# Raw weight blocks in the cached pages' buffers, and 30 turns of the identity, at the start of a hybrid decoder step

## The chip, the core and the metric

The kernel runs on one core of a Trainium2 chip. The core has five engines that run at the same time and wait for one another through semaphores: TensorE (PE in the profile, with its weight loads as PEld), VectorE (DVE), ScalarE (ACT), GpSimd (POOL), and SyncE (SP), which issues most of the transfers between the chip's memory and the core's own buffers. The metric is the device time of one execution in microseconds, lower is better.

## The reference, cut to what matters

One decoder layer is computed for a prompt of 1024 tokens and for 64 sample tokens (8 sequences of 8) that attend to 8192 cached positions each. Its beginning is a norm, one combined projection whose columns are split, and the low-rank latents:

```
n = rmsnorm(h, lw['g_mix'])
u = n @ lw['w_in']
gq, gk, gv, gg, ga, mq, mkv, mkr = jnp.split(u, split_points, axis=-1)
...
cq = rmsnorm(mq, lw['mla_g_qa'])
qf = (cq @ lw['mla_w_qup']).reshape(B, T, MLA_HEADS, MLA_NOPE + MLA_ROPE)
...
ckv = rmsnorm(mkv, lw['mla_g_kva'])
krope = rope(rmsnorm(mkr, lw['mla_g_kr']), pos)
```

The columns `ga, mq, mkv, mkr` are the last 432 of `w_in` (16 + 256 + 128 + 32); the program calls them the latents. After this come gated linear attention and latent attention, whose sample part runs over the paged cache, then an output projection, a gated MLP with a causal convolution, and a gated per-layer embedding.

## The kernel before

Every product is computed in float32 accuracy out of two halves: a value is cast to a rounded high half (`act.copy`) and the remainder is the low half (a subtraction on DVE or POOL); three matmuls (high by high, high by low, low by high) make one product. A weight therefore comes in four steps: a transfer into a raw buffer, a cast on ACT, a subtraction on DVE or POOL, and only then the matmuls.

The program is written as generators that are advanced in turns: the dense work of the prompt in two halves of 512 tokens (`prompt_half`), and the sample sequences' attention over the cached pages. A scheduler then fixes the order of instructions on each engine at build time, by program order, by priority (`tc.high_priority` raises the sample's q chain) and by when buffers come free. Each engine runs its list strictly in that order, so an instruction that waits holds all behind it on its engine. SP can hold eight transfers under way; a ninth waits for the first to land.

The beginning of the first half does this. `sample_x` (L335) loads the 64 sample rows (tile `xin_s`) and the gains `gmix`, normalises the rows and turns them on TensorE (`pt`, L132) into `xTs`. `load_x` (L751) loads the prompt's rows in tiles of 128, the first two into `lat`, the next two into `xin`; each is squared and summed on ACT (L122), scaled by POOL (L108, L111) and DVE (L125), turned on TensorE (L132) and split into `xTh` and `xTl` (L115, L116). `load_lat` (L259) brings the latents' weights in eight blocks of 128 by 432: a raw tile (`stage`, three buffers), a cast to `w` on ACT (L267), a subtraction (L271) on POOL for odd blocks and on DVE for even ones, into `chl` or `w`. `sample_u` (L343) multiplies the sample rows by them: 16 matmuls into `ps_sm`. `proj_lat` multiplies each of four prompt tiles by them: 24 matmuls into `ps_lt` for each (both at L278).

Then comes the sample's q chain: the latents' norm, `ps_qs` (L390), sums and norms on ACT and DVE (L163 to L331), the turns `pt_q` (L416), `ps_qp` (L420), `pt_qr` (L426), and on POOL the operands of the paged attention (L484 to L491). Beside it runs `mix`: chunks of 128 columns of `w_in` (`ps_pj`, L139 to L141), whose raw halves go through the same three `stage` buffers. The paged attention turns pages (`craw`, three buffers of 128 by 1024) into `ctp` and `ks`; `csq` (two buffers of 128 by 1024) holds its squares.

Of the kernel before, what the change touches and what calls it, by code (L numbers as in the profile page):

```python
# [8 lines left out]
F32 = mybir.dt.float32  # L9
# [9 lines left out]
P = 128  # L19
# [20 lines left out]
NL = 432  # L40
# [4 lines left out]
def step_kernel(ctx: ExitStack, tc: tile.TileContext, A):  # L45
    nc = tc.nc
    pe, act, dve, pool, sp = nc.tensor, nc.scalar, nc.vector, nc.gpsimd, nc.sync
# [4 lines left out]
    def ctile(shape, dt, name):  # L52
        return const.tile(shape, dt, name=name, tag=name)
# [3 lines left out]
    ident = ctile([P, P], F32, "ident")  # L57
# [18 lines left out]
    def load_constants():  # L76
        for nm in gains:
            sp.dma_start(gains[nm], A[nm][0].partition_broadcast(P))
        dve.scalar_tensor_tensor(gqk, gains["mla_g_qn"], SCALE, gains["mla_g_kn"], ALU.mult, ALU.mult)
        dve.tensor_scalar(gains["mla_g_qr"], gains["mla_g_qr"], SCALE, None, ALU.mult)  # L80
        sp.dma_start(ropes, A["rope_s"])
# [37 lines left out]
    def norm_rows(wk, x, rows, gb, out=None):  # L119
        junk = wk.tile([P, D], BF16, tag="sqd", name="junk", bufs=1)  # L120
        ss = wk.tile([P, 1], F32, tag="ss", name="ss")
        act.activation(junk[:rows], x, AF.Square, scale=1.0 / 32.0, accum_out=ss[:rows])  # L122
        r = rstd(wk, ss[:rows], rows, 1)
        out = x if out is None else out
        dve.scalar_tensor_tensor(out, x, r[:rows, 0:1], gb[:rows], ALU.mult, ALU.mult)  # L125
        return out

    def transpose_split(ps, xs, rows, put, here=False):
        for c0 in (0, 4):
            pt = ps([P, 4, P], "pt")  # L130
            for c in range(4):
                m = pe.transpose(pt[:, c, :rows], xs[:rows, (c0 + c) * P:(c0 + c + 1) * P], ident[:rows, :rows])  # L132
                if here and c0 == c == 0:
                    tc.keep_in_program_order(m)
            hi, lo = put(c0)
            split(hi, lo, pt[:, :, :rows])
# [47 lines left out]
    cp = ph1.enter_context(tc.tile_pool(name="cp", bufs=1, side="right"))  # L184
# [7 lines left out]
    def pm(shape, name):  # L192
        return psM.tile(shape, F32, tag="m", name=name)

    def cst(shape, dt, name):
        return cp.tile(shape, dt, name=name, tag=name)
# [6 lines left out]
    chl = [cst([P, 9, 258], F32R, "chl")]  # L203
# [28 lines left out]
    wp = den.enter_context(tc.tile_pool(name="wp", bufs=3))  # L232
# [4 lines left out]
    def wtile():  # L237
        return wp.tile([P, 2 * D], F32R, tag="w", name="w")
# [17 lines left out]
        hl = wload(wp, w_in[:, c0:c0 + P], 8, P, "w", sbufs=3, lo_eng=lo_eng, out=(w[:, :, 0], w[:, :, 1]))  # L256
        return hl + (w,)

    def load_lat(first, lo_eng=pool):  # L259

        w = [wtile()[:, 0:4 * NL].rearrange("p (k c) -> p k c", c=NL) for _ in range(3)]
        hi = [w[k // 4][:, k % 4] for k in range(8)]
        lo = first + [w[2][:, k] for k in range(4)]
        for k in range(8):
            raw = wp.tile([P, NL], F32, tag="stage", name="stage", bufs=3)
            sp.dma_start(raw, w_in[k * P:(k + 1) * P, O_GA:O_GA + NL])
            act.copy(hi[k], raw)  # L267
            r, h_ = raw, hi[k].bitcast(F32)
            if len(lo[k].shape) == 3:
                r, h_ = (x.rearrange("p (a c) -> p a c", a=2) for x in (r, h_))  # L270
            (lo_eng if k % 2 else dve).tensor_tensor(lo[k], r, h_, ALU.subtract)  # L271
        return hi, lo
# [63 lines left out]
    def sample_x():  # L336
        x = wk.tile([P, D], F32, tag="xin", name="xin_s")
        sp.dma_start(x[:R], A["x_sample"].rearrange("b t d -> (b t) d"))
        sp.dma_start(gmix, A["g_mix"][0].partition_broadcast(P))
        norm_rows(wk, x[:R], R, gmix)  # L340
        transpose_split(pm, x, R, lambda c0: (xTs[:, c0:c0 + 4, 0:R], xTs[:, c0:c0 + 4, R:2 * R]))

    def sample_u(u, w):  # L343
        ps = pm([P, 512], "ps_sm")
        for k in range(8):
            for s in range(2):
                mm_lat(ps[:, :NL], xTs[:, k, :], w[s][k], k + s == 0, k + s == 8)
        fold_rows(wk, ps, NL, u[:R], "st", 3)
        pt = pm([P, 512], "pt_us")
        pe.transpose(pt[:16, :R], u[:R, 0:16], ident[:R, :R])  # L350
        act.copy(gaTs, pt[:16, :R])
        sp.dma_start(dga[1:17, T:], gaTs)
        sp.dma_start(dga[0:1, T:], ones64[0:1, 0:R])
# [372 lines left out]
    def prompt_half(hf):  # L726
# [26 lines left out]
        def load_x():  # L753
            t = len(loaded)
            if hf == 0 and t < 2:
                x = lat[:, 2 * t:2 * t + 2, :].rearrange("p a c -> p (a c)")
            else:
                x = wk.tile([P, D], F32, tag="xin", name="xin")
            sp.dma_start(x, A["x_prompt"][0, t * P:(t + 1) * P, :])
            loaded.append(x)  # L760
# [13 lines left out]
                xs_.append(norm_rows(wk, x, P, gmix))  # L774

        if hf == 0:
            sample_x()
            load_x()
            wl = load_lat([chl[0][:, 2 * k:2 * k + 2, 0:NL // 2] for k in range(4)])
            load_x()  # L780
            load_constants()
            u = wk.tile([P, NL], F32, tag="u", name="u_s")
            sample_u(u, wl)
# [20 lines left out]
        if hf == 0:  # L804
            with tc.high_priority(SP):
                q = sample_q(cqT, wqe)
                WkT = absorb_weights()
            proj_lat(3, wl)
            with tc.high_priority(SP):
                sample_absorb(q, WkT)  # L810
            yield -1.0
        else:
            xl = [wk.tile([P, D], F32R, tag="xin", name="wlt") for _ in range(2)]
            wl = load_lat([x[:, k * NL:(k + 1) * NL] for x in xl for k in range(2)])
            for i in range(4):
                proj_lat(i, wl)
                yield 4.4
# [546 lines left out]
    def dense():  # L1364
        for hf in range(2):
            z["part"] = 2 * hf
            if hf:
                z["gla"] = gla_weights()
            yield from prompt_half(hf)
        den.close()  # L1370
        wa2 = const.tile([17, 256], F32, tag="gtile", name="wa2")
        sp.dma_start(wa2[0:1], A["gla_b_a"])
        sp.dma_start(wa2[1:17], A["gla_w_a2"][0])
        with ExitStack() as s2:
            g, g2 = (s2.enter_context(tc.tile_pool(name=nm, bufs=2, reuse_waits="tile")) for nm in ("g", "g2"))
            z["part"] = 4
            sample = gla_sample(g, wa2, *z["gla"])
            for n, w in enumerate(gla_prompt(g2, wa2, *z["gla"])):
                yield w
                if n > GS0:  # L1380
                    z["part"] = 5
                    w2 = next(sample, None)
                    if w2 is not None:
                        yield w2
            for w in sample:
                yield w
        with ExitStack() as s2:
            ap = s2.enter_context(tc.tile_pool(name="ap", bufs=2, reuse_waits="tile"))
            z["part"] = 6
            yield from prompt_attention(ap)  # L1390
        z["part"] = 7
        wo_room()
# [870 lines left out]
```

## Time and profile before

| what | value |
| --- | --- |
| time, median of 3 runs | 2215.05 us (2214.86 to 2217.98) |
| span of the profiled execution | 2211.1 us |
| what the median run has beside that span | 3.95 us |
| PE, DVE, ACT, POOL busy | 96%, 75%, 62%, 56% of the span |
| span with no PE instruction running | 84.4 us (2211.1 less 2126.7) |
| first matmul | 8.08 us after the span's start |

The profile lists no time of its own for the profiled execution beside its span; launch and end lie outside it, and the median of the runs is 3.95 us above. In the rows of the timeline the first number is the start in microseconds from the span's start, the second the duration, then engine, line of the program, operation, what is written and what is read, and in brackets how long the engine had been idle and what released it. A matmul's duration overlaps with the next one's; its true step is the distance between the starts of neighbours.

### The profile page before, as it was taken

Reading aid. Unit: us, or ns where it says so; the run is one execution under the profiler, and the core shown is the slowest. Engines: PE = TensorE matmul, PEld = TensorE weight load, DVE = VectorE, ACT = ScalarE, POOL = GpSimd, SP = SyncE. Lnnn points to the kernel's source line nnn. Section 1 sums busy time; section 2 is a strip of 40 time slices with the busy share of each in tenths; the row PEclk is TensorE's granted clock in tenths of the full one; section 3 lists DMA queues with packets and bytes.
Section 4 is the critical chain, followed back from the end, with each engine's and each line's share of the span. In section 5 each row is a group of like instructions: output and inputs, shape, how many; then the busy total and the mean of one; then the engine's idle time right before and its main releaser. Section 6 shows DMA issues by size and latency. Waiting matters only on the chain.

```text
span 2211.1 us, 38379 instructions
## 1 busy us (share of the span) xinstructions
PE 2126.7 (96%) x13460; PEld 1927.2 (87%) x13460; DVE 1668.4 (75%) x2551; ACT 1366.7 (62%) x3724; POOL 1233.9 (56%) x1330
## 2 busy tenths in 40 slices
PE   7999989999999999999999997999999999999999
PEld 6889978878888888887898875999999999888899
DVE  4775667467788888887888788888888886887642
ACT  5676766777778888887777766333333333534631
POOL 5675668576777777778455557756566562011100
PEclk9999999999999999999999998999999999999999
DMA  5343235412342222221522222332232325777321
GB/s 185 106 144 108 78 119 156 141 54 69 105 120 61 63 74 61 61 56 46 171 77 69 74 77 82 101 102 90 92 95 91 101 91 191 240 218 237 101 71 39
DMA packets 204418, 233.07 MB, mean 105 GB/s; under 512 B 42422, under 2 KB 146339, under 8 KB 204227
## 3 DMA queue, kind: packets, MB, share of 16 engines
q1 hardware_dynamic: 188259, 179.49, 26.0%
q0 software_dynamic: 14736, 46.67, 7.4%
q10 hardware_dynamic: 1232, 4.46, 0.5%
q8 instruction: 108, 1.77, 0.3%
q14 instruction: 83, 0.68, 0.1%
HBM read 188.00 MB, written 42.52 MB: 104 GB/s over the span
## 4 chain that ended last, share of the span: by engine, by line
PE 79%; DVE 7%; ACT 5%; DMA 3%; POOL 3%; issue 2%; SPq 0%; DVEq 0%; POOLq 0%; ACTq 0%
PE ps_gu L140 7%; PE ps_gu L141 7%; PE ps_gu L139 7%; PE ks L139 5%; PE ks L141 4%; PE ks L140 4%; PE ps_dn L140 3%; PE ps_dn L141 3%; PE ps_dn L139 3%; PE cpv L646 2%; PE ctp L522 2%; PE ps_lt L278 2%; PE ps_pj L139 2%; DVE css L565 1%; PE ps_pj L140 1%
## 5 line engine op out<-in xcount | busy, mean ns | idle before, releaser
L560 ACT ACTIVATE csq<-ks 128x256 f32<-128x256 f32 x1040 | 392.7, 400 | 91.1 <-PE ks L141 80.2
L565 DVE TENSOR_REDUCE css<-csq 128x16 f32<-128x1024 f32 (+1 forms) x264 | 315.7, 1196 | 61.2 <-ACT csq L560 58.2
L115 ACT CAST wh<-st 128x512 fp32r<-128x512 f32 x176 | 108.4, 619 | 189.0 <-PE ps_gu L140 168.7
L139 PE MATMUL ks<-mv0h,cTh 128*128 128x320 f32 (+1 forms) x520 | 171.0, 331 | 8.8 <-ACT sn L562 4.6
L139 PE MATMUL ks<-mv1h,cTh 128*128 128x320 f32 (+1 forms) x520 | 169.6, 328 | 7.8 <-ACT sn L562 3.5
L605 POOL TENSOR_TENSOR chl<-craw,chl 128x1024 fp32r<-128x1024 f32 x64 | 141.6, 2213 | 55.2 <-ACT chl L603 53.0
L140 PE MATMUL ks<-mv1l,cTh 128*128 128x320 f32 (+1 forms) x520 | 153.1, 296 | 0.0
L140 PE MATMUL ks<-mv0l,cTh 128*128 128x320 f32 (+1 forms) x520 | 152.0, 294 | 0.0
L141 PE MATMUL ks<-mv0h,cTl 128*128 128x320 f32 (+1 forms) x520 | 147.6, 297 | 0.9 <-DVE cTl L116 0.8
L141 PE MATMUL ks<-mv1h,cTl 128*128 128x320 f32 (+1 forms) x520 | 148.0, 298 | 0.1
L116 DVE TENSOR_TENSOR wl<-st,wh 128x512 fp32r<-128x512 f32 x132 | 119.0, 903 | 26.3 <-ACT wh L115 26.3
L631 POOL TENSOR_TENSOR phl<-sn,phl 128x512 fp32r<-128x512 f32 (+1 forms) x64 | 85.5, 1335 | 84.8 <-ACT phl L630 84.3
L116 POOL TENSOR_TENSOR wl<-st,wh 128x512 fp32r<-128x512 f32 x44 | 69.4, 1578 | 102.9 <-ACT wh L115 102.9
L140 PE MATMUL ps_dn<-o 128*128 128x512 f32 x308 | 120.1, 390 | 0.4 <-DVE o L116 0.4
L141 PE MATMUL ps_dn<-o 128*128 128x512 f32 x308 | 120.2, 390 | 0.0
L116 DVE TENSOR_TENSOR cTl<-ctp,cTh 128x512 fp32r<-128x512 f32 (+1 forms) x136 | 90.0, 662 | 37.8 <-ACT cTh L115 36.8
L139 PEld LDWEIGHTS ks<-mv0h,cTh 128*128 128x128 f32 x520 | 97.9, 188 | 23.2 <-ACT sn L562 9.4
L562 ACT COPY sn<-ks 128x64 f32<-128x64 f32 x520 | 116.7, 224 | 0.0
L139 PEld LDWEIGHTS ks<-mv1h,cTh 128*128 128x128 f32 x520 | 99.0, 190 | 20.1 <-ACT sn L562 7.9
L1318 POOL TENSOR_TENSOR pl<-p,ph 128x512 fp32r<-128x512 f32 (+1 forms) x96 | 97.5, 1020 | 30.3 <-DVE ph L1317 21.2
L139 PE MATMUL ps_dn<-o 128*128 128x512 f32 x308 | 112.1, 390 | 0.0
L141 PE MATMUL ps_gu<-xrh,wl 128*128 128x320 f32 x352 | 108.7, 309 | 0.0
(670 smaller groups left out, 7871.4 us busy)
## 6 DMA issues: line engine op xcount, KB each, us to landing
raw<-ds SPq DMA_DIRECT2D x77, 256.0 KB
raw<-ffn_w_down SPq DMA_DIRECT2D x66, 256.0 KB
stage<-w_in SPq DMA_DIRECT2D x48, 256.0 KB
st<-ffn_w_gate SPq DMA_DIRECT2D x44, 256.0 KB
st<-ffn_w_up SPq DMA_DIRECT2D x44, 256.0 KB
wr<-ffn_w_down SPq DMA_DIRECT2D x44, 256.0 KB
ds<-cv SPq DMA_DIRECT2D x21, 512.0 KB
oraw<-doT SPq DMA_DIRECT2D x16, 256.0 KB
```

What stands on the lines that cost most here:

```text
L115: cast = act.copy(hi, src)
L116: res = (lo_eng or dve).tensor_tensor(lo, src, hi.bitcast(F32), ALU.subtract)
L139: pe.matmul(ps, ah, bh, start=first, stop=False)
L140: pe.matmul(ps, ah, bl, start=False, stop=False)
L141: return pe.matmul(ps, al, bh, start=False, stop=last)
L278: pe.matmul(ps, x, w, start=first, stop=last)
L560: act.activation(sq[:, f * 256:f * 256 + 256], ks[:, 0:256], AF.Square)
L562: act.copy(o.sn[:, g0 + i, :], ks[:, 256:320])
L565: dve.tensor_reduce(o.ss[:, g0 + i + 1 - n:g0 + i + 1, :].rearrange("p i h -> p (i h)"), sq2[:, :n].rearrange("p i (h n) -> p (i h) n", n= ...
L605: pool.tensor_tensor(ch[:, c0:c1, 128:256], src, ch[:, c0:c1, 0:128].bitcast(F32), ALU.subtract)
L631: pool.tensor_tensor(phl[:, :nt, 64:128], sb, phl[:, :nt, 0:64].bitcast(F32), ALU.subtract)
L1318: pool.tensor_tensor(pl[:, c0:], p[:, c0:], ph[:, c0:].bitcast(F32), ALU.subtract)
```

## The change

Two things are edited, both at the beginning of the first half. First, TensorE turns the identity matrix 30 times into a PSUM tile (`pt_warm`) that nothing reads. Second, `load_lat` takes a list of rooms: its eight raw blocks no longer share the three `stage` buffers but get a place each, two in every one of the three `craw` buffers and two in a `csq` buffer, which the paged attention does not use yet at that time.

```diff
-    def load_lat(first, lo_eng=pool):
+    def load_lat(first, lo_eng=pool, rooms=None):
...
-            raw = wp.tile([P, NL], F32, tag="stage", name="stage", bufs=3)
+            raw = rooms[k] if rooms else wp.tile([P, NL], F32, tag="stage", name="stage", bufs=3)
...
         if hf == 0:
+            pt = pm([P, 4, P], "pt_warm")
+            for c in range(30):
+                pe.transpose(pt[:, c % 4], ident, ident)
             sample_x()
             load_x()
-            wl = load_lat([chl[0][:, 2 * k:2 * k + 2, 0:NL // 2] for k in range(4)])
+            rooms = [cp.tile([P, 8, P], F32, tag="craw", name="lraw", bufs=3).rearrange("p a c -> p (a c)") for _ in range(3)]
+            rooms.append(cp.tile([P, 2, 512], F32, tag="csq", name="lraw2", bufs=2).rearrange("p a c -> p (a c)"))
+            wl = load_lat([chl[0][:, 2 * k:2 * k + 2, 0:NL // 2] for k in range(4)],
+                          rooms=[x[:, a:a + NL] for x in rooms for a in (0, 512)])
```

The lines behind it stand 3 or 6 lower in the changed file (L839 becomes L845). The scheduler then orders the work anew. In the lists on SP, the eight block transfers now stand in a row behind the first prompt tile and ahead of the second; before, three stood there and the other five came later, one by one, as `stage` buffers came free. The order on the engines differs up to the end of the sample's attention, mostly by some ten places back or forth; from there to the end (about the second half of TensorE's list) it is the same as before.

The opening on TensorE, before (`xin_s` are the sample's rows, `lat` the first two prompt tiles):

```order
L132 MATMUL pt<-ident,xin_s 128x64 x8
L278 MATMUL ps_sm<-w,xTs 128x432
L278 MATMUL ps_sm<-chl,xTs 128x432
L278 MATMUL ps_sm<-w,xTs 128x432
L278 MATMUL ps_sm<-chl,xTs 128x432
L278 MATMUL ps_sm<-w,xTs 128x432
L132 MATMUL pt<-ident,lat 128x128 x8
L278 MATMUL ps_sm<-chl,xTs 128x432
L278 MATMUL ps_sm<-w,xTs 128x432
L132 MATMUL pt<-ident,lat 128x128 x4
L278 MATMUL ps_sm<-chl,xTs 128x432
L132 MATMUL pt<-ident,lat 128x128 x4
```

And now:

```order
L779 MATMUL pt_warm<-ident 128x128 x30
L132 MATMUL pt<-ident,xin_s 128x64 x8
L132 MATMUL pt<-ident,lat 128x128 x8
L278 MATMUL ps_sm<-w,xTs 128x432
L278 MATMUL ps_sm<-chl,xTs 128x432
L278 MATMUL ps_sm<-w,xTs 128x432
L278 MATMUL ps_sm<-chl,xTs 128x432
L278 MATMUL ps_sm<-w,xTs 128x432
L278 MATMUL ps_sm<-chl,xTs 128x432
L278 MATMUL ps_sm<-w,xTs 128x432
L278 MATMUL ps_sm<-chl,xTs 128x432
L278 MATMUL ps_sm<-w,xTs 128x432 x8
```

The first prompt tile's turns moved ahead of all `ps_sm`, and all 16 `ps_sm` stand together ahead of the second tile's turns. On ACT the same stretch stood like this before:

```order
L122 ACTIVATE junk,ss<-lat 128x1024
L267 CAST w<-stage 128x432
L115 CAST xTs<-pt 128x4x64
L267 CAST w<-stage 128x432
L115 CAST xTs<-pt 128x4x64
L267 CAST w<-stage 128x432
L122 ACTIVATE junk,ss<-lat 128x1024
```

And now:

```order
L122 ACTIVATE junk,ss<-lat 128x1024
L267 CAST w<-lraw 128x432 x4
L115 CAST xTs<-pt 128x4x64 x2
L267 CAST w<-lraw 128x432 x2
L115 CAST xTh<-pt 128x4x128
L267 CAST w<-lraw_230 128x432
L115 CAST xTh<-pt 128x4x128
L267 CAST w<-lraw_230 128x432
L122 ACTIVATE junk,ss<-lat 128x1024
```

All eight casts of the latents' weights, and the first tile's `xTh`, now stand ahead of the second tile's square (the last row). The second place is the end of the latents on TensorE. Before, `pt_q` stood behind the whole first chunk of `mix`:

```order
L139 MATMUL ps_pj<-xTh,w 128x512
L140 MATMUL ps_pj<-xTl,w 128x512
L141 MATMUL ps_pj<-xTh,w 128x512
L286 MATMUL ps_sm<-w,xTs 128x256 x4
L416 MATMUL pt_q<-ident,qt 64x64 x8
L839 MATMUL pt_gvs<-ident,gsf 128x64
L854 MATMUL pt_ga<-ident,lat 16x128 x4
L910 MATMUL pt_cq<-ident,lat 128x128 x3
L420 MATMUL ps_qp<-qT_s,WkT 128x64 x8
```

And now it stands behind the first two matmuls of that chunk:

```order
L278 MATMUL ps_lt<-w,xTh 128x432 x2
L278 MATMUL ps_lt<-w,xTl 128x432
L139 MATMUL ps_pj<-xTh,w 128x512
L140 MATMUL ps_pj<-xTl,w 128x512
L416 MATMUL pt_q<-ident,qt 64x64 x8
L141 MATMUL ps_pj<-xTh,w 128x512
L139 MATMUL ps_pj<-xTh,w 128x512
```

The eight `ps_qs` at the head of that chain stood ahead of the last 9 of the 96 `ps_lt` before, and stand ahead of the last 48 now; the eight turns of `pt_wk` (L408) moved from the first chunk of `mix` into the last `ps_lt`. The third place is POOL behind that, where a row of L116 with a 128x4x128 tile is the subtraction for half a chunk of `mix`. Before:

```order
L116 TENSOR_TENSOR w<-stage,w 128x4x128
L108 TENSOR_SCALAR rs_v<-ss_850 128x3
L108 TENSOR_SCALAR rs_v<-ss_871 128x3
L111 TENSOR_TENSOR rs_r<-rs_v,mhalf 128x3 x2
L116 TENSOR_TENSOR w<-stage,w 128x4x128
L484 CAST mv0h<-qp 128x32 x2
L484 CAST mv1h<-qp 128x32 x2
L485 TENSOR_TENSOR mv0l<-qp,mv0h 128x32 x2
```

And now:

```order
L484 CAST mv0h<-qp 128x32 x2
L484 CAST mv1h<-qp 128x32 x2
L490 CAST qbd0h<-qr_113 32x64 x4
L490 CAST qbd1h<-qr_113 32x64 x4
L485 TENSOR_TENSOR mv0l<-qp,mv0h 128x32 x2
L485 TENSOR_TENSOR mv1l<-qp,mv1h 128x32 x2
L491 TENSOR_TENSOR qbd0l<-qr_113,qbd0h 32x64 x3
L473 DMA krraw<-cache_krope,idx 128x256
L116 TENSOR_TENSOR w<-stage,w 128x4x128
L491 TENSOR_TENSOR qbd0l<-qr_113,qbd0h 32x64
L491 TENSOR_TENSOR qbd1l<-qr_113,qbd1h 32x64 x2
L116 TENSOR_TENSOR w<-stage,w 128x4x128
```

The second chunk's two subtractions stood ahead of the attention's operands (L484 to L491) and now stand among them.

## The prediction

> **What bounds the kernel now.** I read the page first, then the chain of waits through the opening, then busy time by stages, then the timeline row by row.
>
> ```profile
> span 2211.1 us, 38379 instructions
> PE 2126.7 (96%) x13460; PEld 1927.2 (87%) x13460; DVE 1668.4 (75%) x2551; ACT 1366.7 (62%) x3724; POOL 1233.9 (56%) x1330
> 3.97 6.99 DMA lat<-x_prompt
> 11.45 5.07 DMA stage<-w_in
> 20.00 3.96 PE ps_lt L278 x12
> 28.39 5.10 PE ps_lt L278 x26
> 43.15 1.41 PE ps_qs L390 x8
> 44.56 1.59 PE ps_lt L278 x8
> ```
>
> TensorE is busy for 96% of the span, so time can come only from the 84.4 us in which it is not, or from stretches in which it is busy but slow. The chain shows both at the opening: it hangs on transfers until 16.5 us, and 12 of the latents' matmuls then take 3.96 us (0.33 each), while later 26 take 5.10 (0.196).
>
> ```profile
> 16.58:20.00 3.42, 2.85 (x11) 2.59 (x12) 2.52 (x4) 3.42 (x8) 1.91 (x3) 1.00 1.09 366
> 20.00:23.41 3.41, 3.41 (x12) 3.10 (x11) 3.41 (x6) 2.83 (x7) 2.04 (x4) 1.00 0.59 160
> 23.41:26.82 3.41, 3.41 (x22) 3.21 (x21) 2.27 (x3) 1.46 (x4) 2.17 (x1) 1.00 0.40 113
> 50.72:54.13 3.41, 3.02 (x20) 2.44 (x18) 2.04 (x2) 2.52 (x12) 3.24 (x6) 1.00 0.91 291
> 54.13:57.54 3.41, 0.26 (x5) 0.29 (x6) 3.34 (x9) 2.06 (x9) 2.95 (x4) 1.00 0.53 170
> 57.54:60.96 3.42, 2.58 (x16) 1.45 (x13) 3.42 (x10) 2.26 (x10) 1.52 (x1) 0.50 0.44 148
> 60.96:64.37 3.41, 3.41 (x16) 3.38 (x16) 3.12 (x15) 1.83 (x4) 3.08 (x4) 0.50 0.36 91
> 64.37:67.79 3.42, 3.42 (x9) 2.65 (x9) 3.31 (x13) 1.12 (x2) 1.85 (x5) 0.50 0.29 71
> ```
>
> These are busy times by stage (PE first; the third number from the end is the granted clock). TensorE's clock is halved in stretches of 3.41 us: an almost idle stretch (0.26 of 3.41) is followed by half speed, and full speed comes back only behind a stretch that was full. Ahead of 23.41 the column says 1.00, but 12 matmuls fit there where 22 fit right behind, so the opening runs at half speed too. The losses I can address: between 8.08 and 46.17 the waits and the slow clock; between 53.7 and 67.8 an idle gap, a small one, and 9.4 us of work at half speed.
>
> **The 30 turns of the identity.**
>
> ```profile
> 1.17 0.29 POOL masks.py:199 TENSOR_SCALAR_AFFINE_SELECT ident<-ident 128x128 f32<-128x128 f32 x1
> 6.75 1.28 DVE L125 SCALAR_TENSOR_TENSOR xin_s<-xin_s,rs_r,gmix 64x1024 f32<-64x1024 f32 x1 [3.08 <-POOL rs_r L111]
> 8.08 1.11 PE L132 MATMUL pt<-ident,xin_s 64*128 64x64 f32 x8 [8.08 <-DVE xin_s L125]
> 17.87 0.85 PE pt L132 x4
> 24.94 0.44 PE pt L132 x4
> ```
>
> The identity is ready at 1.46 us. Thirty turns take 30 x 0.2125 = 6.4 us at half speed, 30 x 0.11 = 3.3 at full speed, so they end between 4.8 and 7.9, before the sample rows arrive at 8.03. They delay nothing; that idle time is their cover. What they bring depends on TensorE staying busy behind them, and the new order has a hole there: the sample's turns end near 8.6, and next in the list are the first prompt tile's turns, whose data are not ready until 12.4 (below). So a gap of 3.8 us follows, longer than one clock stretch. I give the warm-up no gain. If the clock stayed up, the tile's turns and `ps_sm` would end some 1 to 2 us earlier, but the second prompt tile binds at 18.9 in either case, so the doubt is worth something only where that tile comes sooner.
>
> The Trainium skill, "TensorE: Matmul & The Clock Gate", Part 1 (the HAM clock gate), says the array starts at half clock, wakes after a sustained busy window of about 3.4 us that runs freely, and falls back after an idle one. The trace agrees on all three (3.41 us stretches, the idle one at 54.13). By that rule the turns before a 3.8 us hole are wasted and the first term below stays as it is; did the clock outlast the hole, that term would come out at its upper bound of 5.
>
> **The opening, engine by engine.** Durations come from these rows.
>
> ```profile
> 8.03 1.06 ACT L122 ACTIVATE junk<-lat 128x1024 bf16<-128x1024 f32 x1 [2.30 <-DMA lat<-x_prompt]
> stage<-w_in SPq DMA_DIRECT2D x8, 216.0 KB
> 9.58 0.57 POOL L111 TENSOR_TENSOR rs_r<-rs_v,mhalf 128x1 f32<-128x1 f32 x1
> 9.65 0.61 DVE L271 TENSOR_TENSOR chl<-stage,w 128x432 fp32r<-128x432 f32 x1 [1.63 <-ACT w L267]
> 9.79 0.55 ACT L267 CAST w<-stage 128x432 fp32r<-128x432 f32 x1
> 10.25 0.37 ACT L115 CAST xTs<-pt 128x256 fp32r<-128x256 f32 x1
> 10.42 1.11 POOL L271 TENSOR_TENSOR chl<-stage,w 128x432 fp32r<-128x432 f32 x1 [0.27 <-ACT w L267]
> 10.51 2.10 DVE L125 SCALAR_TENSOR_TENSOR lat<-lat,rs_r,gmix 128x1024 f32<-128x1024 f32 x1
> 12.67 1.97 PE L132 MATMUL pt<-ident,lat 128*128 128x128 f32 x8
> 20.11 1.28 DVE L125 SCALAR_TENSOR_TENSOR xin<-xin,rs_r,gmix 128x1024 f32<-128x1024 f32 x1
> ```
>
> ACT squares the first tile from 8.03 to 9.2, casts four blocks (4 x 0.55) to 11.4, then `xTs` (2 x 0.37) to 12.1. DVE subtracts one block, then scales the tile from 10.3; beside POOL's subtraction this takes 2.10 instead of 1.28, so to 12.4. TensorE turns the tile from 12.4 to 14.4 at half speed, then runs 16 `ps_sm`. The last block's cast stands behind two more casts, `xTh`, a cast and `xTh`, so it ends at about 15.5, and POOL's subtraction (1.11) at 16.7. `ps_sm` ends between 17.0 (fast, waiting for that block) and 20.2 (16 x 0.36 behind 14.4); full speed returns after the first full stretch behind 12.4, so I take 18.5. The blocks land in time: before, x rows, gains and three blocks moved until 10.96 (the chain's first DMA row); five more blocks of 216 KB at the same rate, 2.4 MB in about 8 us, add 3.6 us, so the second tile lands near 14.6, and ACT reaches its square only at 15.6. That one ends at 16.8, POOL's part at 17.6, DVE's 1.28 at 18.9. So the second tile's turns run from 18.9 to 19.8, when before they ended at 20.0, but with all 16 `ps_sm` done instead of 8, and at full speed.
>
> What is left then: 96 `ps_lt` x 0.196 = 18.8, 16 turns x 0.11 = 1.8, `ps_qs` 1.4, `pt_wk` 0.9, some small turns 0.6: 23.5 us, ending at 43.3. Before, the same work without `pt_wk` ended at 46.17, so 47.1 with it. **First term: 3.8 us gained.** Bounds: 1 (`ps_sm` at 20.2, the second tile 2 us later than I think) to 5 (the clock up, and DVE's 2.10 a 1.28, so that the second tile comes sooner).
>
> **The q chain and the second chunk.**
>
> ```profile
> 43.89 0.48 ACT L163 COPY sn<-ps_qs 64x384 f32<-64x384 f32 x1
> 51.08 1.03 PE L408 MATMUL pt_wk<-ident,wkr 128*64 128x128 f32 x8
> 57.28 0.80 PE L416 MATMUL pt_q<-ident,qt 64*64 64x64 f32 x8 [3.54 <-DVE qt L328]
> 60.86 3.67 PE L420 MATMUL ps_qp<-qT_s,WkT 64*128 64x64 f32 x16 [0.84 <-ACT qT_s L417]
> 65.94 1.28 POOL L116 TENSOR_TENSOR w<-stage,w 128x512 fp32r<-128x512 f32 x1 [1.63 <-ACT w L115]
> 69.65 1.67 POOL L490 CAST qbd0h<-qr 32x64 fp32r<-32x64 f32 x4 [0.96 <-ACT qr L427]
> ```
>
> From the first sum of `ps_qs` to `pt_q` passed 13.4 us, which 9 `ps_lt` and the first chunk could not cover: 3.54 idle, 0.84 more at `ps_qp`, and half of the 9.4 slow us, 4.7. Together 9.1 us lost. Now 48 `ps_lt` (9.4), `pt_wk` (0.9) and two `ps_pj` (0.5) stand between: 10.8 us of cover. If the chain takes 13.4 again, `pt_q` still waits 2.6; some of the 13.4 were weight casts that now stand behind it, so I take 1.
>
> What is late next is the second chunk. The first one with `pt_q`, `ps_qp` and `pt_qr` keeps TensorE for 9 us, to about 53.5. Its successors need POOL: the operands `mv0l` and `qbd` (some 1.3 us of small casts, then 1.67 for each four of `qbd`), and the second chunk's subtraction (1.28) stands among them; its transfer waits for `stage` buffers that DVE frees behind the q chain. I put 4 us of waiting there and 1 us for a slow stretch. Loss 6 instead of 9.1. **Second term: 3.1 us gained**; bounds from a gain of 7 (only `pt_q`'s small waits) to a loss of 6 (the hole as long as before, 10 us, with three slow stretches, 15 in all).
>
> **The attention behind it.**
>
> ```profile
> 75.00:300.00 225.00, 215.25 (x1397) 197.02 (x1396) 148.85 (x261) 155.26 (x494) 139.11 (x148) 0.98 0.35 111
> 300.00:500.00 200.00, 189.10 (x1224) 164.66 (x1223) 128.94 (x215) 142.58 (x433) 144.33 (x187) 0.98 0.38 115
> 500.00:1020.00 520.00, 508.59 (x3612) 444.51 (x3610) 427.45 (x713) 437.47 (x1340) 382.50 (x415) 1.00 0.26 74
> ```
>
> No instruction is added there, but neighbours change places up to the end of the sample's attention. TensorE idles 9.75 + 10.9 + 11.4 = 32 us in it, and none of these waits has to stay as it is. **Third term: 0**, bounds 4 either way, an eighth of that idle time. Behind it the order is the old one.
>
> **Sum.** 3.8 + 3.1 + 0 = 6.9 us off the span of 2211.1, so 2204.2; with the 3.95 us that the median run has beside that span, 2208.1. A change under 0.2% (4.4 us, so 2210.6 to 2219.5) could not be told from none.
>
> **Rivals.**
>
> The lead is given back (same). The second chunk's hole costs the 9.1 us that the old one did, and the first term is 2 because the raw blocks delay the second tile: 2213. For it: the opening gains only if what follows is not itself waiting for POOL and `stage`; against it: the sample chain starts ten microseconds earlier relative to the dense work. Chance 0.29.
>
> A new hole makes it slower. Place: TensorE between the first and the second chunk of `mix`, where POOL's list has the attention's operands ahead of the weights. If `qp` reaches POOL not at about 51 but 6 us later, TensorE idles 10 us there, the clock falls for three stretches, and 15 us are lost instead of 9.1; with a first term of 2 and 3 lost to the permuted attention, 2215.05 + 5.9 - 2 + 3 = 2222. It decides against the change once hole and slow clock together cost over 12.9 (9.1 + 3.8). For it: POOL's order; against it: high halves and eight more `ks` need none of those subtractions. Chance 0.15.
>
> The hole stays shut (faster still). `pt_q` is ready in time and TensorE fills up with `ks`: second term 7, so 2204.2. For it: the cover of 10.8 us; against it: DVE frees `stage` late. Chance 0.12.
>
> **How the numbers follow.** My forecast keeps 0.44. Faster: 0.44 + 0.12 = 0.56; same 0.29; slower 0.15. The range runs from 2200.5 (the last rival with most of the third term's 4) to 2217.5 (the first rival with 4 more); the forecast's own is 2205 to 2211.
>
> **What would show it.** Right: turns of the identity over by 8; a TensorE gap of 3 to 4 us before the first tile's turns; the second tile's turns at about 19; the last `ps_lt` near 43; no gap of 3.5 us ahead of `pt_q`. Wrong: no gap and full speed from 8 us on; a last `ps_lt` behind 45; over 5 us idle between 53 and 62; or a difference that arises between 75 and 1020 us.

## The result, and the profile after

The changed kernel takes 2225.57 us (median of 4 runs, 2223.65 to 2229.04), the kernel before beside it 2214.95 (2213.76 to 2217.98). The ratio is 1.0043, with a 95% interval of 1.0031 to 1.0055: slower by 9.5 us by the ratio (10.6 between the two medians), where I forecast 2208.1 and a range of 2200.5 to 2217.5.

One number has to be set right first. Each run's time is 1.75 us above its span (2223.65 with a span of 2221.9), so most of the 3.95 us that stood "beside the span" before was a profiled execution 2.2 us quicker than its median. The sum against the median is not changed by that.

The page of the changed kernel, its span and its busy time:

```profile
span 2221.9 us, 38473 instructions
PE 2134.5 (96%) x13490; PEld 1932.0 (87%) x13490; DVE 1682.0 (76%) x2551; ACT 1367.6 (62%) x3724; POOL 1233.2 (55%) x1330
```

10.8 us more span, of which TensorE is busy 7.8 (30 turns are 5 of them), and idle 87.4 us instead of 84.4. TensorE in the opening (timeline; start, duration, line, tile, idle time ahead of it):

```profile
1.51 4.97 PE L779 MATMUL pt_warm<-ident 128*128 128x128 f32 x30 [1.51 <-POOL ident masks.py:199]
8.35 0.71 PE L132 MATMUL pt<-ident,xin_s 64*128 64x64 f32 x8 [1.87 <-DVE xin_s L125]
12.26 1.97 PE L132 MATMUL pt<-ident,lat 128*128 128x128 f32 x8 [3.20 <-DVE lat L125]
21.04 1.09 PE L132 MATMUL pt<-ident,lat 128*128 128x128 f32 x8 [1.70 <-DVE lat L125]
46.81 0.35 PE L278 MATMUL ps_lt<-w,xTl 128*128 128x432 f32 x1
```

The turns are over at 6.5, the gap of 3.20 us follows, and the first tile's turns run at half speed (1.97 for what takes 1.09 later). The trace's clock records have full speed from 4.6 to 11.4 and half from 11.4 to 18.2; TensorE was busy for 3.09 of 3.40 us in the stretch ahead of the rise and for 0.71 of 3.40 in the one ahead of the fall. The Trainium skill, "TensorE: Matmul & The Clock Gate", Part 1, has full speed follow a busy window and half speed an idle one; the trace agrees, though its idle stretch was not quite empty. The second tile comes at 21.04, not at 18.9, and the latents end at 47.0, where the kernel before would with `pt_wk`. VectorE shows why the tile is late, before and after:

```profile
15.97 0.23 DVE L79 SCALAR_TENSOR_TENSOR gqk<-gtile 128x64 f32<-128x64 f32 x1 [1.75 <-DMA gtile<-mla_g_kn]
```

```profile
19.56 0.23 DVE L79 SCALAR_TENSOR_TENSOR gqk<-gtile 128x64 f32<-128x64 f32 x1 [1.80 <-DMA gtile<-mla_g_kn]
19.70 1.28 DVE L125 SCALAR_TENSOR_TENSOR lat<-lat,rs_r,gmix 128x1024 f32<-128x1024 f32 x1
```

The tile's scale factor was ready at 17.8 (POOL), but VectorE stood in front of an operation on the gains, whose transfer now queued behind all eight blocks and came 3.6 us later than before. That the end of the latents hangs on this tile is another matter; the run with the gains moved, below, speaks against it.

To find the rest I compared the two traces at equal work: the matmuls of both are the same 13460 (the 30 turns left out); each got its usual step as weight, and for each moment of the trace before I looked up when the other trace had done the same weight. Positive is later:

| moment before, us | 46 | 60 | 76 | 300 | 425 | 475 | 850 | 1020 | 1420 | end |
| --- | --- | --- | --- | --- | --- | --- | --- | --- | --- | --- |
| changed kernel, us | 0.0 | -5.3 | -2.1 | -4.8 | -4.5 | +0.6 | +2.2 | +7.9 | +11.2 | +10.9 |

So the stretch from 46 to 76 gained 2.1 us, and everything was lost behind it, in the attention whose order alone is new. These are single executions: of the four kernels that share this order up to 425 us (the changed one and three of those below), the profiles stand 0.7 to 2.3 us early at 76 us and 2.3 to 5.3 early at 300. Behind 1020 us, where the order is the old one again, the 3.0 us that arise are not shown to be the change's: the kernel before with five or with ten added turns (below) loses 3.2 there against the same profile, with one turn 1.3. In the stretch view, before and after:

```profile
76.00:1020.00 944.00, 911.93 (x6221) 805.20 (x6220) 705.06 (x1187) 734.33 (x2263) 665.29 (x746) 0.99 0.31 91
```

```profile
76.00:1020.00 944.00, 906.99 (x6145) 797.19 (x6143) 702.76 (x1173) 726.25 (x2228) 656.83 (x736) 0.99 0.31 91
```

76 matmuls fewer in the same 944 us. And the lead at equal work was in the wrong work. The dense chain of the prompt, at the ends of its second and third chunk (`pt_gvs`), before:

```profile
76.54 0.27 PE L839 MATMUL pt_gvs<-ident,gsf 64*128 64x64 f32 x1
94.30 0.27 PE L839 MATMUL pt_gvs<-ident,gsf 64*128 64x64 f32 x1
```

and after:

```profile
81.27 0.27 PE L845 MATMUL pt_gvs<-ident,gsf 64*128 64x64 f32 x1
101.29 0.27 PE L845 MATMUL pt_gvs<-ident,gsf 64*128 64x64 f32 x1 [1.66 <-DVE gsf L292]
```

4.7 and 7.0 us late, while the cached pages are ahead: 9 turns of pages (`ctp`) by 76 us where there were 4, 126 by 425 us where there were 122. What comes behind the dense chain is late by as much (that the chain's end is what releases it was not tested apart). On SP, the gates of the first half (`dgg`) and the gated attention's transfer (`gaT`), and TensorE's wait for it, before:

```profile
412.45 3.03 SPq L830 DMA_DIRECT2D dgg<-G  x3
431.70 0.57 SPq L1002 DMA_DIRECT2D gaT<-dga  x1
437.14 0.69 PE L1007 MATMUL ps_z<-wa,gaT 17*128 17x256 f32 x2 [2.23 <-DMA gaT<-dga]
```

and after, with TensorE's stretches and their clock (third number from the end):

```profile
416.96 3.04 SPq L836 DMA_DIRECT2D dgg<-G  x3
436.25 0.47 SPq L1008 DMA_DIRECT2D gaT<-dga  x1
442.27 1.22 PE L1013 MATMUL ps_z<-wa,gaT 17*128 17x256 f32 x2 [3.75 <-DMA gaT<-dga]
438.20:441.50 3.30, 0.33 (x3) 0.06 (x1) 1.22 (x1) 0.84 (x4) 3.06 (x4) 1.00 1.20 195
441.50:444.90 3.40, 2.63 (x8) 1.98 (x9) 0.00 (x0) 0.82 (x3) 0.00 (x0) 0.50 1.10 294
444.90:448.30 3.40, 3.40 (x18) 3.40 (x17) 1.98 (x4) 2.21 (x8) 2.01 (x5) 0.50 0.63 196
```

The wait of 3.75 us empties one of the stretches of 3.41 us in which the clock is granted (0.33 of 3.30), and two at half speed follow. Before, the wait was 2.23 us and the clock stayed up. Length alone does not decide that: at the same place a wait of 1.68 us in the first crossed kernel below and one of 2.02 in the kernel with one turn in the gap were each followed by one stretch at half speed, one of 2.30 in the kernel with the gains moved by none.

### The profile page after: what moved, and what is told of

The parts are those of the page before. It is cut to its first block, busy times and chain, and to the rows that moved or that the text cites. A ratio compares the mean times of both kernels' runs of the same rounds, so it can differ in the third digit from the quotient of the medians.

```text
span 2221.9 us, 38473 instructions
## 1 busy us (share of the span) xinstructions
PE 2134.5 (96%) x13490; PEld 1932.0 (87%) x13490; DVE 1682.0 (76%) x2551; ACT 1367.6 (62%) x3724; POOL 1233.2 (55%) x1330
## 4 chain that ended last, share of the span: by engine, by line
PE 75%; DVE 10%; ACT 5%; POOL 4%; DMA 3%; issue 3%; SPq 0%; DVEq 0%; POOLq 0%; ACTq 0%
PE ps_gu L139 7%; PE ps_gu L141 7%; PE ps_gu L140 7%; PE ks L139 5%; PE ks L141 4%; PE ks L140 4%; PE ps_dn L141 3%; PE ps_dn L140 3%; PE ps_dn L139 3%; PE cpv L646 2%; PE ctp L522 2%; DVE css L565 2%; PE ps_pg L141 1%; PE ps_pg L140 1%; PE ps_pg L139 1%
## 5 line engine op out<-in xcount | busy, mean ns | idle before, releaser
L140 PE MATMUL ks<-mv0l,cTh 128*128 128x256 f32 (+1 forms) x520 | 153.3, 297 | 0.0
L141 PE MATMUL ks<-mv0h,cTl 128*128 128x256 f32 (+1 forms) x520 | 148.7, 298 | 0.8 <-DVE cTl L116 0.7
L116 DVE TENSOR_TENSOR wl<-st,wh 128x512 fp32r<-128x512 f32 x132 | 119.0, 904 | 29.2 <-ACT wh L115 29.2
L116 POOL TENSOR_TENSOR wl<-st,wh 128x512 fp32r<-128x512 f32 x44 | 68.9, 1567 | 105.7 <-ACT wh L115 105.7
L116 DVE TENSOR_TENSOR cTl<-ctp,cTh 128x512 fp32r<-128x512 f32 (+1 forms) x136 | 90.0, 661 | 45.6 <-ACT cTh L115 44.6
L592 POOL TENSOR_TENSOR sn<-sn,cy 128x512 f32<-128x512 f32 (+1 forms) x64 | 70.5, 1102 | 75.5 <-DVE cy L590 63.4
```

The costliest lines, as they stand in the source:

```text
L116: res = (lo_eng or dve).tensor_tensor(lo, src, hi.bitcast(F32), ALU.subtract)
L140: pe.matmul(ps, ah, bl, start=False, stop=False)
L141: return pe.matmul(ps, al, bh, start=False, stop=last)
L592: pool.tensor_tensor(snv, snv, y[:, :nt].rearrange("p i h -> p (i h)").unsqueeze(2).broadcast_to([P, nt * 8, 8]), ALU.mult)
```

## The experiments

Each was timed beside the kernel before on its chip; ratios are to that, and 0.001 is 2.2 us. To hold an order fixed, a kernel lists, for each engine, the places of its instructions in program order, and ties neighbours by edges that set the order of issue and no wait:

```diff
+        for a, b in zip(order, order[1:]):
+            tc.add_manual_dep(b, a.name, how, reason="pin")
```

**Opening or order: two kernels crossed.** The first takes the changed kernel's opening and the old order behind it, the second the reverse. Theory A says that the order costs, theory B the opening, theory C the mismatch.

```diff
         step_kernel(tc, A)
+        pin(tc)
```

> The changed kernel's opening (30 turns, rooms, its own order for the first 296 matmuls and what belongs to them) and behind it, from about 76 us on, the order of the kernel before on all five engines. Theory A (the permuted order of the attention costs the time: at equal work the changed kernel was 2.2 us ahead at 76 us of the kernel before, and 11 us behind at 1410): about 2213, so 0.9990 of before, between 2211 and 2216. Theory B (the opening itself, its late second tile and the weights that POOL takes after the operands, is what costs): 2225 as the whole change. Theory C (any order fixed for other arrival times stalls, so neither opening nor order alone): between 2216 and 2222.

Measured: 1.0005 (0.9996 to 1.0013), 2215.7 us, at the upper end of theory A's range.

> The reverse: the kernel before without turns and rooms, and behind its first 310 matmuls the order of the changed kernel on all five engines. Theory A: 2215 + 10.6 of the whole change + 2.2 that the opening gained = 2228, between 2224 and 2230. Theory B: 2215, as before. Theory C: between 2216 and 2224.

Measured: 1.0058 (1.0046 to 1.0070), 2228.1 us, theory A's number. At equal work this kernel is 1.2 us late at 76 us and 11.1 at 1020, and it has the wait of the changed kernel:

```profile
PE ps_z L1007 <- DMA gaT<-dga: 3.3, 1, 3.3
```

So the cost sits in the order behind 76 us. The opening brought nothing to the end either (A had 2213, the interval allows down to 2214).

**The two edits apart**, their order free again.

```diff
-            pt = pm([P, 4, P], "pt_warm")
-            for c in range(30):
-                pe.transpose(pt[:, c % 4], ident, ident)
```

> The eight rooms without the 30 turns; the order on the engines is free and comes out different again from both. Theory A: the opening is as quick as in the changed kernel (a lead of 1 to 3 us at 76 us), and the total is open by as much as such an order moved it before, 2205 to 2227; what it is decides nothing but the size of that spread. Theory B (the rooms cost): 2225.

Measured: 1.0083 (1.0070 to 1.0096). The rooms alone, which put yet another order on 7386 of 13094 matmuls, lose twice as much, more than either theory had. The rooms themselves are not the cause: the first crossed kernel has them too, under the old order.

The second is the kernel before with the turns added:

```diff
+            pt = pm([P, 4, P], "pt_warm")
+            for c in range(30):
+                pe.transpose(pt[:, c % 4], ident, ident)
```

> The 30 turns without the rooms; the order is free, and differs from that of the kernel before in 2171 of 13094 matmuls, by 15 places on the mean, where the whole change moves 6121. Theory A: no lead at 76 us (0 to 1 us), the total within 2210 to 2220 and away from 2215 only by what arises behind 76 us. Theory B with the turns as the cause: 2225.

Measured: 0.9994 (0.9985 to 1.0003): the turns alone change nothing that can be told.

**The second tile's wait.** The two operations on the gains are tied behind the second tile's scaling; opening otherwise as in the changed kernel, old order behind.

```diff
+                    for x in scaled:
+                        tc.add_manual_dep(x.ins, last.name, mybir.DependencyInfo(
+                            mybir.DependencyClass.NoSync, mybir.DependencyReason.DATA), reason="behind the second tile")
```

> As the first kernel here (new opening, old order behind it), but VectorE's two operations on the gains (gqk, L79, and L80) stand behind the scaling of the second prompt tile, which in the changed kernel waits 1.80 us behind them for a transfer of gains. Theory D (that wait is why the second tile's turns began at 21.0 instead of the predicted 18.9): turns at 19.3, last ps_lt 1.7 us sooner, about 45.3; if such a lead is kept, 2214.0, against 2215.7 of the first kernel. Theory E (whatever the opening gains is given back in the wait ahead of the second chunk, 58 to 68 us): 2215.7, with the last ps_lt sooner and equal work at 76 us not.

Measured: 0.9994 (0.9984 to 1.0003), 0.0011 under the first crossed kernel, but the two intervals overlap. The turns came at 19.34 instead of 21.04, so the wait named is what made the second tile late. The end of the latents did not follow. The last `ps_lt` started at 46.69, against 46.81 in the changed kernel; five kernels with this opening unedited have it between 46.03 and 48.15, and the first crossed kernel's 48.15 is the latest of them. The lead of 1.70 us had shrunk to 0.74 by the fourth tile's turns (32.90 against 33.64), and the q chain's first matmuls, which wait for VectorE's `cqT_s` 0.81 us here, started at 35.06. In the changed kernel:

```profile
35.18 1.15 PE L390 MATMUL ps_qs<-wqe,cqT_s 128*128 128x384 f32 x5 [0.51 <-DVE cqT_s L116]
```

**Holding the clock over the gap.** 26 more turns between the sample's turns and the first tile's.

```diff
+            for c in range(26):
+                GAP.append(tc.keep_in_program_order(pe.transpose(pt[:, c % 4, :], ident, ident)).ins.name)
```

> As the kernel with the gains moved, and 26 more turns of the identity between the turns of the sample rows and those of the first prompt tile, over the 3.2 us gap after which the clock fell. Expected of the clock: no half speed between 11.4 and 18.2 us, the first tile's turns in 1 us instead of 2, ps_sm done near 17 instead of 19.3. Theory D (the second tile binds whatever the clock does): the last ps_lt as in the kernel with the gains moved, total within 1 us of it. Theory F (the slow clock of the opening is what costs): 2.3 us more gained, 2211.7.

Measured: 1.0044 (1.0033 to 1.0056), and no test of it: the tile of the turns held one of two PSUM buffers, so the sample's last four turns waited.

```profile
13.85 0.69 PE L133 MATMUL pt<-ident,xin_s 64*128 64x64 f32 x4 [5.17 <-DVE xTs L117]
```

The last `ps_lt` started at 50.48, 3.8 us later than with the gains moved alone, but the kernel lost 11. This comes back below.

**Where in the new order.** Two kernels follow the changed kernel's order up to a point (its 2430th and its 5030th matmul) and the old one for what is left; only the fixed lists differ.

> The changed kernel with its own order for its first 2430 matmuls (to about 425 us, where at equal work it was 4.5 us ahead of the kernel before) and what belongs to them on the other engines, and the order of the kernel before for all that is left. Theory A (each order has its own stalls at its own places): the lead stays, 2215.5 - 4.5 = 2211, between 2209 and 2213. Theory C (an order fixed for other arrival times stalls): 2215 to 2222.

Measured: 1.0010 (0.9999 to 1.0021), about 2217.2 and in theory C's range, so the lead did not stay. It went at one place:

```profile
436.24 1.22 PE L1013 MATMUL ps_z<-wa,gaT 17*128 17x256 f32 x2 [6.08 <-DMA gaT<-dga]
```

TensorE arrives sooner and waits longer: it came 4.7 us sooner than in the kernel before (430.2 against 434.9), the transfer landed only 0.9 sooner (436.2 against 437.1). The 4.5 us at equal work were pages done early, and the gated attention does not wait for pages.

> The same with the changed kernel's order up to its 5030th matmul, about 852 us, where it was 2.2 us behind, and the old order for the rest. Theory A: what was lost between 425 and 475 us stays lost, the 6 us that were lost between 850 and 1020 come back: 2217.5, between 2216 and 2220. Theory C: 2220 to 2228. If the loss between 850 and 1020 hangs on what arrives there and not on the order there: 2225.

Measured: 1.0035 (1.0021 to 1.0048), about 2222.7, in theory C's range and between the two other numbers. The profile is 6.2 us late at 850 and 9.7 at 900, although the old order rules from 852; behind 900 it loses no more until 1020. So theory A in its simple form (each stretch has its own loss) falls: part of what is lost behind 850 hangs on what was done before it.

**The wait itself.** Theory G: the 8 us lost from 430 to 460 are the wait for `gaT` and the clock behind it. On SP that one transfer moves ahead of three transfers of `Ss`, the gated attention's stored states; four places of SP's fixed list change, and the order is otherwise untouched. First on the changed kernel.

> The changed kernel with its own order everywhere, but on SP the first transfer of gates for the gated attention (gaT, L1008), for which TensorE waited 3.75 us at 438 to 442 us, stands ahead of the last three transfers of Ss (L1104), 2.1 us sooner. Theory G (of the 8 us lost between 430 and 460 us most is this wait and the half clock that follows it, 441 to 448 us): the wait is 1.6 us or none, the clock falls once less, so 2.1 to 5.5 us less than the changed kernel: 2219 to 2222.5, likeliest 2219. Rival (the dense work is late there anyway, so something else is waited for): 2225.

Measured: 1.0009 (1.0000 to 1.0018), 2218.15 us. From 1.0043 that is 7.5 us back, more than the 2.1 to 5.5 that theory G had; at equal work 6.7 of them arise between 430 and 475 us. The wait is gone and the clock stays up:

```profile
440.98 0.69 PE L1013 MATMUL ps_z<-wa,gaT 17*128 17x256 f32 x2
438.20:441.50 3.30, 3.19 (x20) 2.50 (x20) 1.95 (x4) 3.19 (x13) 3.30 (x8) 1.00 0.97 231
441.50:444.90 3.40, 3.02 (x22) 2.65 (x21) 2.08 (x3) 2.21 (x8) 3.40 (x6) 1.00 1.14 229
```

Then on the kernel with the turns alone, where the wait was 3.26 us:

> The kernel with the turns alone, its own order, and the same one transfer moved on SP. There the wait was 3.26 us, with half speed behind it. Theory G: 2213.7 less 2 to 5 us: 2209, between 2207.5 and 2212, faster than both kernels. Rival: 2213.7.

Measured: 0.9971 (0.9960 to 0.9981), 2209.37 us: faster than both kernels by 6 and 16 us, as theory G had it. And on the kernel with the gains moved:

> The kernel with the gains moved (new opening, old order), and the same transfer moved on SP ahead of the last two of Ss, 1.4 us sooner. The wait was 1.7 us without half speed behind it. Theory G: 2213.6 less 1 to 1.7 us: 2212.3. Rival: 2213.6.

Measured: 1.0015 (1.0006 to 1.0024), 4.6 us slower than without the move and above both expectations. Its wait of 2.30 us for `gaT` is gone too, but TensorE then meets the pages' statistics before POOL is done with them:

```profile
PE mt L618 <- POOL ml L600: 3.1, 1, 3.1
```

That wait was 0.8 us without the move, so the sum of the two is what it was, 3.1 us, but now in one piece: the clock was at half speed for two stretches behind it (445.7 to 452.6), and without the move for none. At equal work this place cost 2.1 us more than without the move; what makes the rest of the 4.6 was not traced. So the cure is one of the place and not of the transfer: the next wait can take over.

**Holding the clock again**, with the turns in a PSUM buffer of their own.

```diff
+            pg = psK.tile([P, 512], F32, tag="k", name="pt_gap").rearrange("p (a c) -> p a c", c=P)
```

> The 26 turns in the gap once more, now into a PSUM buffer of the paged attention's pool. In the earlier run of this idea the tile of the first 30 turns kept one of two PSUM buffers, so that the sample's second four turns waited 5.17 us and the opening came 3.8 us late; its price is no answer to the question. All else, and the order on every engine, as in the kernel with the gains moved. Theory D (the second tile binds): no half speed before 20 us, the first tile's turns in 1 us, ps_sm done near 17, the second tile's turns at 19.3 as without them, total 0.9994 of before, within 1 us of that kernel. Theory F (the slow clock of the opening costs): 2 us less than that kernel, 0.9985.

Measured: 1.0037 (1.0023 to 1.0051). In the opening theory D holds: the clock stays up, and the second tile's turns wait for it all the same.

```profile
8.62 3.06 PE L784 MATMUL pt_gap<-ident 128*128 128x128 f32 x26
12.28 1.09 PE L133 MATMUL pt<-ident,lat 128*128 128x128 f32 x8 [0.60 <-DVE lat L126]
18.72 1.09 PE L133 MATMUL pt<-ident,lat 128*128 128x128 f32 x8 [1.20 <-DVE lat L126]
```

But neither theory's total came: with the order of the kernel with the gains moved on every engine, and a last `ps_lt` 0.6 us from it, it takes 9.5 us more. That left open whether a small shift of arrival can cost so much (theory H) or is carried as it is (K). Four kernels shift TensorE alone, ahead of the second chunk at 64.5 us, in the kernel before with its own order fixed; the one with twenty turns:

```diff
+            for c in range(20):
+                GAP.append((tc.keep_in_program_order if c else (lambda x: x))(pe.transpose(pg[:, c % 4], ident, ident)).ins.name)
```

> The kernel before, its own order fixed on all five engines, and one turn of the identity (0.1 to 0.2 us) on TensorE ahead of the second chunk of mix, 64.5 us. The control for the three that follow. Theory H (what lies behind the opening moves by several us either way for small shifts of arrival): anything from 2211 to 2224. Theory K (a shift is carried to the end as it is): 2215 to 2216.

> The same with five turns, 1.1 us at half speed. Theory K: 2216. Theory H: no relation to 1.1; 2211 to 2224.

> The same with ten turns, 2.1 us at half speed. Theory K: 2217. Theory H: 2212 to 2225, and not in line with the others.

> The same with twenty turns, 4.2 us at half speed, less if the clock comes back in them. Theory K: 2219. Theory H: 2213 to 2230, and not in line with the others.

Measured: 0.9999, 0.9992, 1.0000 and 1.0013 (each within 0.0012 either way), so -0.2, -1.8, 0 and +2.9 us for shifts of about 0.2, 1.1, 2.1 and 4.2. Theory K, or a little less (for five turns its 1.1 us lies just outside the interval); shifts of this size cost no more than themselves at this place, so H is not seen here. The first of them also says that fixing an order costs nothing that these intervals can tell. Two more took the turns in the gap down to one and to thirteen:

```diff
-            for c in range(26):
+            for c in range(13):
```

> The kernel with 26 turns in the opening's gap, with one turn there instead of 26 (gains moved, old order, the same PSUM buffer). If the buffer or the way the order is fixed made that kernel 8 us slower than the one with the gains moved: 2223. If the turns themselves did: 2214 to 2215, as the kernel with the gains moved.

Measured: 1.0004 (0.9995 to 1.0014).

> The same with 13 turns, which fill 1.4 to 2.8 us of the 3.6 us gap. If what costs is the clock held in the opening, and 13 turns hold it too: 2223. If they don't hold it, or the earlier 8 us hang on something else: 2214 to 2215.

Measured: 1.0037 (1.0023 to 1.0051), as with 26. Neither the buffer nor the fixed order, then, but the turns. At equal work the kernels with one and with thirteen turns are level to 0.3 us up to 325 us and 4.2 us apart at 350. There ScalarE waits for a buffer that a store (`dq`) still reads. With one turn and with thirteen:

```profile
340.42 0.37 ACT L952 COPY kt<-ps_kv 128x256 f32<-128x256 f32 x1 [1.25 <-DMA dq<-qt]
```

```profile
342.14 0.37 ACT L952 COPY kt<-ps_kv 128x256 f32<-128x256 f32 x1 [3.11 <-DMA dq<-qt]
```

The store was issued at 338.03 and 337.88. The rate of transfer from 337 to 342.5 us, in 40 slices, first with one turn, then with thirteen, and the second queue that was at work in the latter only:

```profile
GB/s 15 0 52 78 67 127 268 283 354 320 261 97 0 179 402 402 380 357 492 380 268 0 0 0 0 0 0 0 0 0 0 0 0 0 0 0 0 0 0 0
```

```profile
GB/s 0 30 71 45 123 216 287 339 313 302 160 22 320 357 380 357 380 447 380 179 0 0 0 22 0 0 22 0 22 45 22 22 22 0 0 0 0 0 0 0
q8 instruction: 1, 0.02, 1.7%
```

With thirteen turns the store has a tail at 22 GB/s: its last packets go one after another, and they begin when one 16 KB packet of the instruction queue ends (338.8 to 340.3 us in the trace's records). With one turn that packet runs at 343.5, when the store is over. Over the kernels with the old order:

| kernel (old order) | store issued, us | instruction packet, us | ScalarE's wait, us | ratio |
| --- | --- | --- | --- | --- |
| gains moved | 336.71 | 342.3 | 1.24 | 0.9994 |
| one turn in the gap | 338.03 | 343.5 | 1.25 | 1.0004 |
| twenty turns at 64 us | 341.43 | 348.7 | 1.24 | 1.0013 |
| thirteen in the gap | 337.88 | 338.8 | 3.11 | 1.0037 |
| 26 in the gap | 338.06 | 338.9 | 3.24 | 1.0037 |
| 26, with the PSUM wait | 341.99 | 343.9 | 3.51 | 1.0044 |

The wait is longer exactly where the packet falls on the store (before, and in the other kernels with the old order, it is 1.23 to 1.25 as well). In all three the tail's first packet starts within 0.02 us of the instruction packet's end. A rival, that the clock held up in the opening is what moves things, does not fit: with 26 turns and the PSUM wait the clock was at half speed from 11.7 to 18.5, and the long wait is there too. Of the 7.3 us between one turn and thirteen, this place explains the 4.2 that arise by 350, of which 2.2 are left at 375; the rest arises mostly at 700 and behind 1030 and was not traced. So a change of twelve turns can cost several us after all, here not by the shift of arrival but by where an instruction packet falls.

## Why the prediction was wrong, point by point

**The 30 turns**: right, over at 6.5 (4.8 to 7.9), a gap of 3.2 us (3.8), then half speed, no gain.

**First term, 3.8 us gained: wrong, it was 0.** The step that failed is "DVE's 1.28 at 18.9". ACT's square (15.3 to 16.4) and POOL's part (17.8) came as worked out; I followed the queues of those two and not VectorE's, where the gains' operation stood ahead of the tile with a transfer that the eight blocks had delayed. That made the second tile 2.1 us late; the other 1.6 is the work behind it, 25.1 us and not 23.5. A second step failed with it, and the run with the gains moved shows it: with the turns at 19.34 the last `ps_lt` still started at 46.69. "What is left then" was summed as work without a wait, but the q chain's `ps_qs` stands in it and waits for the sample's `cqT_s`; it started at 35.06 and 35.18 with and without the tile's lead. So with the tile in time the term would still have stayed under 1 us (last `ps_lt` at 46.1 to 46.7 in three kernels with the gains moved).

**Second term, 3.1 us gained: TensorE's time nearly right, its meaning wrong.** At equal work the stretch gave 2.1 us (0.9 to 2.1 in the profiles of the four kernels that share this order). The step "Loss 6 instead of 9.1" counted idle time and slow clock only. The hole was filled with pages, and the second chunk ended 4.7 us later than before.

**Third term, 0, bounds 4 either way: the term that was mis-sized.** From 76 us to 1020 the changed kernel lost 10.0 us, and 3.0 more to the end, which executions of the kernel before with a few added turns lose as well. The crossed kernels show it as the order's (+12.8 us with the old opening), and moving one transfer shows 7.5 us of it as the wait for `gaT` with the clock's fall. "An eighth of that idle time" was no bound: a wait can cost more than itself when the clock falls behind it (3.75 us of wait, 7.5 us back; 3.26 and about 5 in the kernel with the turns alone), and work that is reordered between two chains moves the end of the one that others wait for. With what was measured the sum is 0 - 2.1 + 10.0 + 3.0 = +10.9, the span's +10.8.

**The rivals.** "A new hole makes it slower" gave 2222 and the right side, but not by its mechanism: between 58 and 68 us TensorE idled 3.9 us with one slow stretch, not 10 with three. Its observation (POOL's operands ahead of the weights) was where the dense chain fell behind: the second chunk's two subtractions started at 68.0 and 71.0 us, before at 59.4 and 65.9, although their casts were done at 62.1 and 63.9 and POOL was at the operands and a page transfer until 68.0. It became a delay of that chain and not a hole. "The lead is given back" came nearest to the first crossed kernel (1.0005). The four signs that I named for being wrong included the two that came: a last `ps_lt` behind 45, and a difference that arises between 75 and 1020 us.

**What stays open.** Why the second chunk's order came out as it did is the scheduler's, and was not tried. What is lost between 850 and 1020 (5.7 us, in waits each under 1.4) was not settled: the three kernels with the new order there lose 5.6 to 5.8 whether they arrive 1.8 us early or 5.4 late, but the kernel with the old order from 852 on lost 3.5 as well. And the 3.0 us behind 1020 leave the comparison of single profiles no finer than that.

## What to carry to other kernels

An edit in a program that a scheduler orders anew is two edits, and the second can be larger: fix both orders and cross the new opening with the old order before explaining either. Do not bound what a reordering costs by idle time, and do not read a lead at equal work as progress: ask which chain the next wait hangs on, and whether that chain is ahead. When a transfer is added, follow every engine's list to the operation that waits for a transfer behind it, the idle-looking engine's too. And measure a step that an edit speeds up where it ends, over several executions: 1.7 us at the second tile were 0.1 at the end of the latents.

## What the runs showed of the hardware that I had not expected

Instructions are transfers too. Each of these traces has 108 packets of 16 KB on the instruction queue, about 1 us each; when one fell on a store of 384 KB, the store's last packets came 1.9 us later, and ScalarE's wait for it rose from 1.25 to 3.1 to 3.5 us in all three kernels where they met. Twelve turns more in the gap moved the packet from 343.5 to 338.8 us; why by that much is open. The Trainium skill, "Runtime: NRT & Kernel Launch", section "Instruction fetch mechanics", says that instructions are fetched in blocks of 16 KiB by a DMA queue of the sequencer's own, and calls the cost mostly hidden. The size and the queue agree with the trace; the cost here is that of the transfer it meets, and was not hidden.
